# Two encoder layers on one core: the feed-forward input product in Strassen blocks, the output product as a second pass over DRAM

## The chip, the cores and the metric

The kernel runs on one core of one Trainium2 chip. The metric is the device time of one execution in microseconds (us). Engines are TensorE (PE; PEld is its weight load), VectorE (DVE), ScalarE (ACT), GpSimd (POOL) and SyncE (SP, which issues all DMAs of this kernel).

## The reference, cut to what matters

All tensors are float32: 1024 tokens, model width 1024, two layers, feed-forward width 2816.

```python
def conv_ffn(h, w_in, conv_w, conv_b, w_out):          # w_in (1024, 5632), w_out (2816, 1024)
    gu = dwconv_centred(h @ w_in, conv_w, conv_b)      # 3 taps along the tokens, per column, plus bias
    gate, up = split_last(gu, [D_FF, D_FF])
    return (jax.nn.silu(gate) * up) @ w_out
...
    for l in range(DEPTH):
        ...                                            # o: four mixers side by side (attention, scans)
        x = x + rms_norm(o @ w_out[l], post_mix_norm[l])
        h = rms_norm(x, pre_ffn_norm[l])
        x = x + rms_norm(conv_ffn(h, f_w_in[l], f_conv_w[l], f_conv_b[l], f_w_out[l]), post_ffn_norm[l])
```

## The kernel before

One program runs both layers; a layer is the mixers (`mix`), the projection of their output (`out_proj`), and the feed-forward part (`ffn`). Every product of float32 matrices is made of three matmuls on rounded parts: each operand is split into hi (an ACT copy to the fp32r type, L133) and lo (source minus hi, L135, on DVE unless POOL is named), and hi*hi + hi*lo + lo*hi are summed in PSUM. `split` and `splits` do this everywhere, so L133 and L135 are lines of many tiles.

The normalised activations `hn` of a token tile (128 tokens) are transposed on TensorE and split into `hT` (`hT_tile`, L192 to L205): model columns on partitions, tokens along the free axis, in two halves of 512 tokens. Token tiles 0 to 3 are done inside the projection's pipeline; `hn` of tiles 4 to 7 is held and flipped after it (L1463 to L1480).

The feed-forward input product takes the 5632 columns of `w_in` in tiles of 128. For each, `load_T` (L243) loads two raw tiles of 256 KB and splits them, and `gemm_T` (L254) runs 8 row tiles x 3 terms x 2 token halves of matmuls with 512 moving columns into a PSUM tile `pm` of 1024 columns. The first two column tiles of a layer go half by half, so that the first token half is used before the second is there. Column tile f is the gate, 22 + f the matching up tile; `post_gate` and `post_up` run the convolution straight from PSUM (`conv`, L388 to L390: one ACT instruction with tap and bias, two DVE instructions for the neighbours), then tanh on ACT and the gate product (silu as tanh, L320, L321), the product of gate and up (L328), and the split of the result in 256-column parts `gh`, `gl` in SBUF.

The output product is interleaved: after every two pairs, `out_tile` (L348) adds their part of all 8 token tiles, six matmuls of 512 columns for each half of the model width, into two one-bank PSUM tiles, and DVE adds these to the accumulator `acc` (L362). The last group runs through `skew`, a software pipeline, with the layer's tail behind it: `postnorm` (L207), and in the first layer the next layer's `prenorm`, transposes and first column work.

Tiles in SBUF come from pools with tags: `s4` (4 KB per partition, 34 of them), `s2`, `s1`, and `raw` (4 tiles for incoming weights). PSUM has 2 tiles `p2` of two banks, 2 `p1` and 2 `pt` of one bank. A tile waits until one of its tag is free. The instruction order on each engine is set when the program is built, by a planner that takes the instructions in the order in which the code names them as priorities and its own durations; on the chip each engine takes its instructions strictly in that order, and SP its DMA issues too.

```python
class Trunk:
    slots = 34, 12, 24          # s4, s2, s1
...
    def splits(self, *parts, eng=None):
        nc = self.nc
        for hi, lo, src in parts:
            nc.scalar.activation(out=hi, in_=src, func=AF.Copy)
        for hi, lo, src in parts:
            (eng or nc.vector).tensor_tensor(lo, src, hi.bitcast(F32), op=ALU.subtract)
```

## Time and profile before

| | us |
|---|---|
| median of three runs (3164.81 to 3168.3) | 3168.2 |
| the profiled execution, its own time | 3163.46 |
| span of the profiled execution, first to last instruction | 3161.7 |
| TensorE busy in it | 2988.0 |
| mean granted TensorE clock, share of full speed | 0.976 |

The span is read from the trace of the profiled execution. Busy time of an engine is the time in which at least one of its instructions runs; TensorE's matmuls overlap, so the mean duration of one is longer than the distance from one to the next. In the trace, the feed-forward part of layer 1 lies between about 857 and 1600 us, that of layer 2 between about 2420 and the end.

### The profile page before, as it was taken

The numbers are of one execution on the slowest core, as the hardware profiler recorded it, in microseconds if no ns is written. First come the engines' busy times: TensorE is split into PE (matmuls) and PEld (weight loads), VectorE is DVE, ScalarE is ACT, GpSimd is POOL, SyncE is SP. The second block draws the span as 40 slices with busy tenths as digits, with TensorE's granted clock in tenths as the row PEclk, the third lists the DMA queues.
The fourth block names the chain that finished last, engine by engine and source line by source line (L and its number), as shares of the span: only waits on it lengthen the run. The fifth ranks groups of instructions, "written<-read, shape, count | busy, mean of one in ns | idle before, by whom it ended". The sixth has DMA issues, their size and how long they took to land. (4 is left out here: it accounts for less than half of the span.)

```text
span 3161.7 us, 48962 instructions
## 1 busy us (share of the span) xinstructions
PE 2988.0 (95%) x18206; PEld 2493.7 (79%) x18206; DVE 1941.6 (61%) x3654; ACT 1262.7 (40%) x2695; POOL 793.3 (25%) x1257
## 2 busy tenths in 40 slices
PE   6998998999999999999999988999899999999997
PEld 6777776777888888888787777777788888888886
DVE  4556587696545555555565574887955455555556
ACT  3333355785432222222243333577744322222221
POOL 1256667221200000000143675763211000000003
PEclk9999998999999999999999998999999999999999
DMA  4246533233321111111232545232422111111212
GB/s 138 66 144 156 130 88 88 77 102 99 110 66 41 50 59 53 40 41 60 77 126 77 158 131 134 81 92 73 116 94 98 54 57 61 44 40 43 62 36 113
DMA packets 384977, 266.76 MB, mean 84 GB/s; under 512 B 148288, under 2 KB 353636, under 8 KB 384740
## 3 DMA queue, kind: packets, MB, share of 16 engines
q1 hardware_dynamic: 384740, 263.64, 28.7%
q8 instruction: 144, 2.36, 0.3%
q14 instruction: 93, 0.76, 0.1%
HBM read 194.54 MB, written 68.94 MB: 83 GB/s over the span
## 5 line engine op out<-in xcount | busy, mean ns | idle before, releaser
L263 PE MATMUL p<-hT,wh 128*128 128x512 f32 x3456 | 960.1, 392 | 7.8 <-ACT cy L388 2.6
L263 PEld LDWEIGHTS p<-hT,wh 128*128 128x128 f32 x3456 | 649.6, 189 | 145.4 <-ACT cy L388 3.4
L263 PE MATMUL p<-hT,wl 128*128 128x512 f32 x1728 | 553.1, 391 | 0.0
L221 POOL TENSOR_TENSOR acc<-acc,gain 128x768 f32<-128x768 f32 x14 | 28.9, 2064 | 1412.5 <-ACT junk L177 1412.5
L263 PEld LDWEIGHTS p<-hT,wl 128*128 128x128 f32 x1728 | 325.3, 189 | 68.3 <-DVE wl L135 0.9
L388 ACT ACTIVATE cy<-p,cw 128x1024 f32<-128x1024 f32 x88 | 106.0, 1204 | 593.8 <-PE p L263 593.8
L389 DVE SCALAR_TENSOR_TENSOR cy<-p,cw,cy 128x1023 f32<-128x1023 f32 x88 | 112.8, 1282 | 362.3 <-ACT cy L388 362.1
L523 PE MATMUL p<-wn,hT 128*128 128x256 f32 (+1 forms) x1920 | 291.6, 307 | 30.8 <-DVE pb L563 15.5
L523 PEld LDWEIGHTS p<-wn,hT 128*128 128x128 f32 x1920 | 267.5, 199 | 40.9 <-DVE pb L563 17.2
L133 ACT ACTIVATE wh<-raw 128x512 fp32r<-128x512 f32 x216 | 128.0, 624 | 184.1 <-PE p L263 94.6
L135 DVE TENSOR_TENSOR pT<-pt,pT 128x512 fp32r<-128x512 f32 x256 | 173.2, 683 | 39.1 <-ACT pT L133 37.8
L133 ACT ACTIVATE pT<-pt 128x512 fp32r<-128x512 f32 x256 | 150.5, 596 | 96.8 <-PE pt L493 86.8
L493 PE MATMUL pt<-ident,p 128*128 128x128 f32 x1024 | 158.2, 280 | 21.9 <-DVE qh L135 8.2
L362 DVE TENSOR_TENSOR acc<-acc,p 128x512 f32<-128x512 f32 x160 | 109.3, 685 | 93.2 <-PE p L358 93.2
L362 DVE TENSOR_TENSOR acc<-acc,pt 128x512 f32<-128x512 f32 x160 | 109.5, 684 | 90.9 <-PE pt L358 88.9
L1087 DVE TENSOR_REDUCE nm<-p 128x1 f32<-128x1024 f32 x128 | 155.1, 1217 | 13.8 <-PE p L1085 13.2
L1420 PE MATMUL p<-wo,oh 128*128 128x512 f32 x512 | 161.7, 394 | 0.8 <-ACT oh L133 0.8
L493 PEld LDWEIGHTS pt<-ident,p 128*128 128x128 f32 x1024 | 117.4, 142 | 49.0 <-DVE qh L135 11.1
L135 DVE TENSOR_TENSOR wl<-raw,wh 128x512 fp32r<-128x512 f32 x180 | 116.5, 686 | 61.8 <-ACT wh L133 61.6
L1093 ACT ACTIVATE p<-p,nm 128x1024 f32<-128x1024 f32 x128 | 142.3, 1112 | 21.9 <-DVE nm L1087 21.0
L358 PE MATMUL p<-owh,gh 128*128 128x512 f32 x352 | 138.1, 392 | 2.7 <-DVE acc L362 2.7
L358 PE MATMUL pt<-owh,gh 128*128 128x512 f32 x352 | 137.7, 391 | 2.9 <-DVE acc L362 2.8
(317 smaller groups left out, 5624.3 us busy)
## 6 DMA issues: line engine op xcount, KB each, us to landing
raw<-in_f_w_in_dram SPq DMA_DIRECT2D x176, 256.0 KB
raw<-in_f_w_out_dram SPq DMA_DIRECT2D x88, 256.0 KB
raw<-in_w_in_dram SPq DMA_DIRECT2D x72, 256.0 KB
raw<-in_w_out_dram SPq DMA_DIRECT2D x32, 256.0 KB
xr<-x_mid SPq DMA_DIRECT2D x16, 512.0 KB
x_mid<-xr SPq DMA_DIRECT2D x14, 512.0 KB
orow<-o_d SPq DMA_DIRECT2D x48, 128.0 KB
pa<-pa_d SPq DMA_DIRECT2D x32, 176.0 KB
```

Source lines behind the costliest of these rows:

```text
L133: nc.scalar.activation(out=hi, in_=src, func=AF.Copy)
L135: (eng or nc.vector).tensor_tensor(lo, src, hi.bitcast(F32), op=ALU.subtract)
L263: nc.tensor.matmul(pm[:, h * 512:(h + 1) * 512], s[:, k % 4, :], self.h_mov(p, k, h), start=a, stop=b)
L358: nc.tensor.matmul(po, s[i // 2][:, tk], w[:, cs], start=a, stop=b)
L362: nc.vector.tensor_tensor(acc[i][:, cs], acc[i][:, cs], po, op=ALU.add)
L388: nc.scalar.activation(out=y, in_=p, func=AF.Identity, scale=w1, bias=b)
L389: nc.vector.scalar_tensor_tensor(y[:, 1:], p[:, :n - 1], w0, y[:, 1:], op0=ALU.mult, op1=ALU.add)
L493: self.nc.tensor.transpose(pt[:n, t, :], src(4 * c + t), self.ident)
L523: self.nc.tensor.matmul(po, self.h_sta(a, k, i), wt[k][b], start=(k == 0 and a == 0 and b == 0), stop=(k == 7 and a == 1))
L1087: v.reduce_max(nm, s, axis=AX.X, negate=True)
L1093: nc.scalar.activation(out=p, in_=s, func=AF.Exp, bias=nm, accum_out=rs)
L1420: nc.tensor.matmul(y[:, cs], s[k // 2][:, k % 2, :], W[k][w][:, cs], start=(k == 0 and s is oh and w == 0), stop=(k == 7 and s is ol))
```

## The change

The input product is done for a pair (gate tile f, up tile 22 + f) at once, as a product of 2 x 2 blocks: the columns of the pair (gate, up) and the two halves of the 1024 model columns on one side (a11, a12, a21, a22, weight blocks of 512 x 128), the two halves of the model columns and the two token halves on the other (11, 21 for the first token half, 12, 22 for the second). Strassen's scheme in Winograd's form needs 7 block products of 4 x 3 matmuls where 8 were used. Its sums come before and after: the sums of activations (T1 to T4) are made once per layer in `block_tile`, the sums of weight blocks (s1 to s4) for each pair in `pair_pieces` on POOL, and the sums of products partly in PSUM (products added into Q and E) and partly by ACT copies and DVE additions into the SBUF tiles `ug` and `uu`. The convolution then reads these. Each weight piece (hi and lo) is an `s4` tile. Products of a pair and the next are interleaved in the order that `order` writes out; pieces are named up to `piece_ahead` products before their use.

The gated product of each pair goes to a DRAM tile `g_d`. After all 22 pairs, the output product runs as a second pass over blocks of feed-forward tiles, 2, then five times 4: `load_out` loads and splits the weights of the next block, `load_g` reads g back and splits it. The first block uses the small `s1` tiles, with matmuls of 256 columns. The last block is in the pipeline with the layer's tail. There are 38 `s4` tiles in place of 34; a scratch area is set to 1024 bytes.

```diff
@@ -52,7 +52,8 @@
     def t(self, pool, shape, dt, tag, **kw):
         return pool.tile(shape, dt, tag=tag, name=self.nm(tag), **kw)
 
-    slots = 34, 12, 24
+    slots = 38, 12, 24
+    piece_ahead = 3
 
     def setup(self):
         nc = self.nc
@@ -284,15 +285,96 @@
         self.drain(prev)
         yield len(jobs)
 
+    def block_tile(self, i, hn):
+        nc = self.nc
+        v, g = nc.vector, nc.gpsimd
+        half, o = divmod(i, 4)
+        sl = slice(o * 128, (o + 1) * 128)
+
+        def operand():
+            return [[self.s4([128, 2, 512], F32R, "H") for _ in range(2)] for _ in range(2)]
+
+        def put(name, src, eng):
+            hi, lo = self.H[name]
+            self.splits(*((hi[k][:, :, sl], lo[k][:, :, sl], src[:, 2 * k:2 * k + 2, :]) for k in range(2)), eng=eng)
+
+        if i == 0:
+            self.H = {n: operand() for n in ("11", "21")}
+            self.Hraw = [[self.s4([128, 2, 512], nm="Hr") for _ in range(2)] for _ in range(2)]
+        if i == 4:
+            self.H.update({n: operand() for n in ("22", "T1", "T2", "T3", "T4")})
+        pts = []
+        for c in range(2):
+            pt = (self.pt, self.p1)[c * half]([128, 4, 128])
+            for k in range(4):
+                nc.tensor.transpose(pt[:, k, :], hn[:, (4 * c + k) * 128:(4 * c + k + 1) * 128], self.ident)
+            pts.append(pt)
+            if half == 0:
+                put(("11", "21")[c], pt, v)
+                for k in range(2):
+                    nc.scalar.activation(out=self.Hraw[c][k][:, :, sl], in_=pt[:, 2 * k:2 * k + 2, :], func=AF.Copy)
+        if half == 0:
+            return
+        b12, b22 = pts
+        old = lambda c: [r[:, :, sl] for r in self.Hraw[c]]
+        cut = lambda t: [t[:, 2 * k:2 * k + 2, :] for k in range(2)]
+        put("22", b22, v)
+        t1, t2, t3, t4 = (self.s2([128, 4, 128], nm="hc") for _ in range(4))
+        for x, y, z in zip(cut(t1), cut(b12), old(0)):
+            v.tensor_tensor(x, y, z, op=ALU.subtract)
+        v.tensor_tensor(t2, b22, t1, op=ALU.subtract)
+        put("T1", t1, v)
+        put("T2", t2, v)
+        nc.scalar.activation(out=t3, in_=b12, func=AF.Copy)
+        v.tensor_tensor(t3, b22, t3, op=ALU.subtract)
+        put("T3", t3, g)
+        for x, y, z in zip(cut(t4), old(1), cut(t2)):
+            g.tensor_tensor(x, y, z, op=ALU.subtract)
+        put("T4", t4, g)
+
+    def load_pair(self, w, f):
+        raws = []
+        for c0, kh in ((f * 128, 0), (D_FF + f * 128, 0), (D_FF + f * 128, 1), (f * 128, 1)):
+            raw = self.t(self.mem, [128, 4, 128], F32, "raw", bufs=4)
+            self.nc.sync.dma_start(raw, w[kh * 512:(kh + 1) * 512, c0:c0 + 128].rearrange("(k p) c -> p k c", p=128))
+            raws.append(raw)
+        return raws
+
+    def pair_pieces(self, raws):
+        nc = self.nc
+        v, g = nc.vector, nc.gpsimd
+        a11, a21, a22, a12 = raws
+
+        def piece(src, eng):
+            w = self.s4([128, 2, 4, 128], F32R, "wp")
+            self.split(w[:, 0], w[:, 1], src, eng)
+            return w
+
+        def combine(x, y, op):
+            t = self.s2([128, 4, 128], nm="wc")
+            g.tensor_tensor(t, x, y, op=op)
+            return t
+
+        s1 = combine(a21, a22, ALU.add)
+        yield piece(a11, v)
+        yield piece(s1, v)
+        s2 = combine(s1, a11, ALU.subtract)
+        yield piece(a12, v)
+        s4 = combine(a12, s2, ALU.subtract)
+        yield piece(s4, v)
+        s3 = combine(a11, a21, ALU.subtract)
+        yield piece(s2, v)
+        yield piece(s3, g)
+        yield piece(a22, g)
+
     def ffn_first(self, l, P):
-        self.ffn_w = self.load_T(P["f_w_in"][l], 0)
+        self.ffn_w = self.load_pair(P["f_w_in"][l], 0)
 
     def ffn(self, l, P, tail):
         nc = self.nc
+        v = nc.vector
         w_in, w_out = P["f_w_in"][l], P["f_w_out"][l]
-        G = 2
-        NG = NFF // G
-        acc = [None] * NT
+        g_d = self.dr.tile([NFF, 128, L], F32, name=self.nm("g_d"), tag="g_d")
...
+        order = [(0, x) for x in (1, 2, 5, 3, 6)]
+        for f in range(NFF):
+            if f + 1 < NFF:
+                order += [(f + 1, 1), (f, 7), (f + 1, 5), (f, 4), (f + 1, 2), (f + 1, 3), (f + 1, 6)]
+            else:
+                order += [(f, 7), (f, 4)]
+        plan = [(f, x) for f in range(NFF) for x in (1, 5, 2, 3, 6, 7, 4)]
+        made, makers, st = {}, {}, {}
+        raws = {0: self.ffn_w}
+        moving = {1: "11", 5: "T1", 2: "21", 3: "22", 6: "T2", 7: "T3", 4: "T4"}
+
+        def ensure(n):
+            while len(made) < n and plan:
+                f, x = plan.pop(0)
+                if f not in makers:
+                    if f not in raws:
+                        raws[f] = self.load_pair(w_in, f)
+                    makers[f] = self.pair_pieces(raws.pop(f))
+                made[f, x] = next(makers[f])
+
+        def finish(f):
+            ug, uu = st.pop(f)[2:4]
+            y = []
+            for c, u in ((f, ug), (NFF + f, uu)):
+                y.append(self.s4([128, L], nm="cy"))
+                self.conv(y[-1], u, *(cw[:, j, c:c + 1] for j in range(4)))
+                if u is ug:
+                    for h in range(2):
+                        hs = slice(h * 512, (h + 1) * 512)
+                        nc.scalar.activation(out=ug[:, hs], in_=y[0][:, hs], func=AF.Tanh)
+                        v.scalar_tensor_tensor(y[0][:, hs], ug[:, hs], 1.0, y[0][:, hs], op0=ALU.add, op1=ALU.mult)
+            v.tensor_tensor(y[1], y[1], y[0], op=ALU.mult)
+            nc.sync.dma_start(g_d[f], y[1])
+
+        for f, x in order:
+            ensure(self.piece_ahead)
+            w = made.pop((f, x))
+            if x == 1:
+                st[f] = [self.p1([128, 512]), self.p2([128, L]), self.s4([128, L], nm="u"), self.s4([128, L], nm="u"), {}]
+            Q, ER, ug, uu, tmp = st[f]
+            E, R = ER[:, 0:512], ER[:, 512:1024]
+            dst = {5: E, 3: E, 2: R}.get(x, Q)
+            hi, lo = self.H[moving[x]]
+            for k in range(4):
+                for s, (a, m) in enumerate(((0, hi), (0, lo), (1, hi))):
+                    nc.tensor.matmul(dst, w[:, a, k, :], m[k // 2][:, k % 2, :], start=(x in (1, 2, 5) and k == 0 and s == 0),
+                                     stop=(k == 3 and s == 2), skip_group_check=True)
+            if x == 2:
+                tmp["c"] = self.s2([128, 512], nm="p1c")
+                nc.scalar.activation(out=tmp["c"], in_=Q, func=AF.Copy)
+                v.tensor_tensor(ug[:, 0:512], tmp["c"], R, op=ALU.add)
+            if x == 5:
+                tmp["e"] = self.s2([128, 512], nm="ec")
+                nc.scalar.activation(out=tmp["e"], in_=E, func=AF.Copy)
+            if x == 6:
+                tmp["u"] = self.s2([128, 512], nm="uc")
+                nc.scalar.activation(out=tmp["u"], in_=Q, func=AF.Copy)
+                v.tensor_tensor(ug[:, 512:1024], tmp["u"], E, op=ALU.add)
+            if x == 7:
+                v.tensor_tensor(uu[:, 512:1024], tmp["e"], Q, op=ALU.add)
+            if x == 4:
+                nc.scalar.activation(out=uu[:, 0:512], in_=Q, func=AF.Copy)
+                finish(f)
+
+        acc = [None] * NT
+        blocks = [range(0, 2)] + [range(i, i + 4) for i in range(2, NFF, 4)]
+
+        def load_out(f, small):
+            parts = []
             for c in range(2):
-                cs = slice(c * 512, (c + 1) * 512)
                 raw = self.t(self.mem, [128, 512], F32, "raw", bufs=4)
...
+                nc.sync.dma_start(raw, w_out[f * 128:(f + 1) * 128, c * 512:(c + 1) * 512])
+                if small:
+                    for q in range(2):
+                        t = self.s1([128, 256], F32R, "owh"), self.s1([128, 256], F32R, "owl")
+                        self.split(*t, raw[:, q * 256:(q + 1) * 256])
+                        parts.append((c, q * 256, 256, *t))
+                else:
+                    if c == 0:
+                        hl = self.s4([128, DM], F32R, "owh"), self.s4([128, DM], F32R, "owl")
+                    t = [x[:, c * 512:(c + 1) * 512] for x in hl]
+                    self.split(*t, raw)
+                    parts.append((c, 0, 512, *t))
+            return parts
+
+        def load_g(fs, i, small):
+            n, w = len(fs), (128 if small else 256)
+            make = (lambda dt, nm: self.s1([128, 2, 128], dt, nm)) if small else (lambda dt, nm: self.s4([128, 4, 256], dt, nm))
+            raw, hi, lo = make(F32, "gr"), make(F32R, "gh"), make(F32R, "gl")
+            nc.sync.dma_start(raw, g_d[fs[0]:fs[0] + n, :, i * 128:i * 128 + w].rearrange("f p t -> p f t"))
+            self.split(hi, lo, raw)
+            return hi, lo
+
+        def out_tile(bi, i, W, G):
+            fs = blocks[bi]
+            small = len(fs) == 2
+            gh, gl = G[i if small else i // 2]
+            tk = slice(0, 128) if small else slice((i % 2) * 128, (i % 2) * 128 + 128)
+            if bi == 0:
                 acc[i] = self.s4([128, DM], nm="acc")
             for c in range(2):
                 cs = slice(c * 512, (c + 1) * 512)
                 po = (self.p1, self.pt)[c]([128, 512])
...
+                for q in range(2 if small else 1):
+                    for j, f in enumerate(fs):
+                        _, o, n, wh, wl = [x for x in W[f] if x[0] == c][q]
+                        for s, (a, b) in enumerate(((gh, wh), (gh, wl), (gl, wh))):
+                            nc.tensor.matmul(po[:, o:o + n], a[:, j, tk], b, start=(j == 0 and s == 0), stop=(j == len(fs) - 1 and s == 2))
+                if bi == 0:
                     nc.scalar.activation(out=acc[i][:, cs], in_=po, func=AF.Copy)
                 else:
-                    nc.vector.tensor_tensor(acc[i][:, cs], acc[i][:, cs], po, op=ALU.add)
+                    v.tensor_tensor(acc[i][:, cs], acc[i][:, cs], po, op=ALU.add)
             return acc[i]
 
...
+        W = {f: load_out(f, True) for f in blocks[0]}
+        for bi, fs in enumerate(blocks):
+            small = bi == 0
+            step = 1 if small else 2
+            nxt = {}
+            G = {}
+
+            def grab(i):
+                if i < NT and i % step == 0:
+                    G[i // step] = load_g(fs, i, small)
+
+            def tile(i, _=None):
+                if i == 0:
+                    grab(0)
+                grab(i + step)
+                if bi + 1 < len(blocks) and i % 2 == 0:
+                    f = blocks[bi + 1][i // 2]
+                    nxt[f] = load_out(f, False)
+                return out_tile(bi, i, W, G)
+
+            if bi + 1 < len(blocks):
+                for i in range(NT):
+                    tile(i)
+            else:
+                self.drain(self.skew(NT, tile, *tail()))
+            W = nxt
 
     def conv(self, y, p, w0, w1, w2, b=None):
         nc = self.nc
@@ -1462,7 +1611,7 @@
 
         def flip(i, hn):
             if i < 4:
-                self.hT_tile(i, hn)
+                self.block_tile(i, hn)
             else:
                 held.append((i, hn))
 
@@ -1477,7 +1626,7 @@
             if k == self.ffn_at:
                 self.ffn_first(l, P)
         for i, hn in held:
-            self.hT_tile(i, hn, 1)
+            self.block_tile(i, hn)
 
         def end():
             gp = self.bcast_row(P["post_ffn_norm"][l])
@@ -1510,7 +1659,7 @@
     import concourse.bacc as _bacc
     from concourse.bass_utils import run_bass_kernel_spmd as _run
 
-    nc = _bacc.Bacc("TRN2", target_bir_lowering=False, num_devices=1)
+    nc = _bacc.Bacc("TRN2", target_bir_lowering=False, num_devices=1, dynamic_dma_scratch_size=1024)
```

## Rows read from the trace of the kernel before

**Rows 1.** The page, busy time of each engine over the span.

```profile
PE 2988.0 (95%) x18206; PEld 2493.7 (79%) x18206; DVE 1941.6 (61%) x3654; ACT 1262.7 (40%) x2695; POOL 793.3 (25%) x1257
```

**Rows 2.** Stretches of feed-forward layer 1: busy us, (instructions), granted clock, DMA share.

```profile
1000.00:1100.00 100.00, 100.00 (x443) 82.81 (x442) 50.20 (x72) 20.32 (x36) 0.00 (x0) 1.00 0.12 38
...
sum 500.00, PE 500.00 PEld 414.01 DVE 269.33 ACT 121.21 POOL 0.00; mean PE 100.00 PEld 82.80 DVE 53.87 ACT 24.24 POOL 0.00
```

**Rows 3.** Groups by line, TensorE: count, busy us, mean ns, idle before.

```profile
L263 PE MATMUL p<-hT,wh 128*128 128x512 f32 x3456 | 960.1, 392 | 7.8 <-ACT cy L388 2.6 <-ACT wh L133 2.2 <-DVE dy L390 1.7
...
L263 PE MATMUL p<-hT,wl 128*128 128x512 f32 x1728 | 553.1, 391 | 0.0
...
L358 PE MATMUL p<-owh,gh 128*128 128x512 f32 x352 | 138.1, 392 | 2.7 <-DVE acc L362 2.7
```

**Rows 4.** Timeline, attention stage, TensorE: 256-wide products (start, length, count).

```profile
410.06 2.15 PE L1118 MATMUL p<-pT,VA 128*128 128x256 f32 x16
```

**Rows 5.** Groups by line: ACT, DVE and POOL durations of the operations that recur.

```profile
L133 ACT ACTIVATE wh<-raw 128x512 fp32r<-128x512 f32 x216 | 128.0, 624 | 184.1 <-PE p L263 94.6 <-DMA raw<-in_f_w_in_dram 52.7 <-issue 17.0
...
L135 DVE TENSOR_TENSOR wl<-raw,wh 128x512 fp32r<-128x512 f32 x180 | 116.5, 686 | 61.8 <-ACT wh L133 61.6
...
L389 DVE SCALAR_TENSOR_TENSOR cy<-p,cw,cy 128x1023 f32<-128x1023 f32 x88 | 112.8, 1282 | 362.3 <-ACT cy L388 362.1
...
L362 DVE TENSOR_TENSOR acc<-acc,p 128x512 f32<-128x512 f32 x160 | 109.3, 685 | 93.2 <-PE p L358 93.2
L388 ACT ACTIVATE cy<-p,cw 128x1024 f32<-128x1024 f32 x88 | 106.0, 1204 | 593.8 <-PE p L263 593.8
...
L321 DVE SCALAR_TENSOR_TENSOR cy<-th,cy 128x512 f32<-128x512 f32 x88 | 56.9, 688 | 31.8 <-ACT th L320 31.8
...
L328 DVE TENSOR_TENSOR cy<-cy,cy 128x1024 f32<-128x1024 f32 x44 | 53.6, 1219 | 0.1
...
L135 POOL TENSOR_TENSOR wl<-raw,wh 128x512 fp32r<-128x512 f32 x36 | 47.7, 1328 | 78.1 <-ACT wh L133 75.0 <-DMA pa_d<-pa 3.0
...
L741 POOL TENSOR_TENSOR X<-xs,dt 128x256 f32<-128x256 f32 x60 | 39.7, 671 | 41.6 <-PE p L767 40.8 <-DVE X L764 0.9
```

**Rows 6.** Timeline, end of layer 1: DVE, POOL and a TensorE wait.

```profile
1570.44 1.85 POOL L221 TENSOR_TENSOR acc<-acc,gain 128x768 f32<-128x768 f32 x1 [706.26 <-ACT junk L177]
...
1570.81 0.69 DVE L362 TENSOR_TENSOR acc<-acc,pt 128x512 f32<-128x512 f32 x1 [1.70 <-PE pt L358]
...
1574.49 2.07 POOL L221 TENSOR_TENSOR acc<-acc,gain 128x768 f32<-128x768 f32 x1 [1.24 <-ACT junk L177]
...
1574.79 2.86 DVE L226 SCALAR_TENSOR_TENSOR xr<-acc,rs,xr 128x1024 f32<-128x1024 f32 x1
...
1577.57 1.27 DVE L362 TENSOR_TENSOR acc<-acc,p 128x512 f32<-128x512 f32 x2
...
1578.30 0.50 PE L358 MATMUL p<-owh,gh 128*128 128x512 f32 x1 [2.04 <-DVE acc L362]
...
1578.76 1.27 DVE L226 SCALAR_TENSOR_TENSOR xr<-acc,rs,xr 128x1024 f32<-128x1024 f32 x1
```

**Rows 7.** Timeline, start of feed-forward layer 1.

```profile
855.71 0.39 PE L1420 MATMUL p<-wo,ol 128*128 128x512 f32 x1
...
857.17 0.70 PE L263 MATMUL p<-hT,wh 128*128 128x512 f32 x2
...
871.14 1.41 DVE L135 TENSOR_TENSOR hT<-p,hT 128x256 fp32r<-128x256 f32 x4
```

**Rows 8.** Stretches at the start and the end of feed-forward layer 1.

```profile
860.00:880.00 20.00, 19.59 (x95) 15.90 (x93) 12.71 (x27) 9.30 (x25) 2.52 (x3) 1.00 0.44 132
...
1570.00:1580.00 10.00, 7.96 (x34) 6.22 (x33) 8.59 (x9) 3.71 (x8) 7.43 (x7) 0.98 0.43 123
1580.00:1590.00 10.00, 7.67 (x33) 6.29 (x32) 9.29 (x10) 4.66 (x10) 8.85 (x12) 0.83 0.54 195
```

**Rows 9.** Timeline, the program's last TensorE instruction.

```profile
3147.69 0.63 PE L358 MATMUL pt<-owh,gl 128*128 128x512 f32 x1
```

More of the change, by code (lines that the diff above doesn't have):

```diff
@@ L324, in post_up @@
-        def post_up(f, pm):
-            y = side(pm, NFF + f)
-            yield
-            g = gate.pop(f)
-            nc.vector.tensor_tensor(y, y, g, op=ALU.mult)
-            gh, gl = [], []
-            for c in range(4):
-                a, b = self.s1([128, 256], F32R, "gh"), self.s1([128, 256], F32R, "gl")
-                self.split(a, b, y[:, c * 256:(c + 1) * 256])
-                gh.append(a)
-                gl.append(b)
-            gT[f] = gh, gl
-        def load_out(f):
-            wh = self.s4([128, DM], F32R, "owh")
-            wl = self.s4([128, DM], F32R, "owl")
+        order = [(0, x) for x in (1, 2, 5, 3, 6)]
@@ L369, in ffn @@
-        per = 2 * G
-        for i in self.run_T(jobs, self.ffn_w):
-            gi, r = divmod(i, per)
-            if r == 0 and gi < NG:
-                for j in range(G):
-                    load_out(gi * G + j)
-            if r == 1 and 0 < gi < NG:
-                for tk in range(NT // 2 if gi == NG - 1 else NT):
-                    out_tile(gi - 1, tk)
-        for tk in range(NT // 2, NT):
-            out_tile(NG - 2, tk)
-        self.drain(self.skew(NT, lambda i, _: out_tile(NG - 1, i), *tail()))
+        W = {f: load_out(f, True) for f in blocks[0]}
```

30 lines of the change are left out of this document (removed).

## The prediction

> **What bounds the kernel now.** I read the page first: TensorE is busy 95% of the span, VectorE (DVE) 61%, ScalarE (ACT) 40%, GpSimd (POOL) 25% [rows 1]. Shares over a span hide stages, so I then took the middle of one feed-forward layer in stretches of 100 us. There TensorE is busy for 500.00 of 500 us at full clock, while DVE has half of its time free, ACT three quarters, and POOL does nothing; the DMA engines are busy 12 to 20% [rows 2]. The reader is to see two things. Only fewer or shorter matmuls can shorten this stage; and the stage has much idle time on the other engines, so work may be added there as long as it does not become the longer queue. The groups by line give the matmul groups concerned, their idle time before is 8 us out of some 1,500 [rows 3]. The pitch follows from the count: 443 matmuls of 512 columns in 100 us, 0.226 us each [rows 2].
>
> **The change on TensorE.** The input product of a layer has 44 column tiles x 8 row tiles x 3 (hi and lo terms) x 2 token halves = 2112 matmuls of 512 columns, the output product 22 x 8 x 2 x 3 = 1056. After the change the input product has 22 pairs x 7 products x 4 x 3 = 1848. The output product keeps its work, but the first block of two tiles runs in 256-column halves: 192 such matmuls in place of 96. So 264 + 96 = 360 matmuls x 0.226 = 81.4 us go. The 256-column ones take (2.15 - 0.28)/15 = 0.125 us each where sixteen of them run in a row [rows 4] (0.28, the length of one, stands at the end of the run); 192 x 0.125 = 24.0 come. Net -57.4 per layer, **-115 us** for both. Nothing hides this: it is the bound itself.
>
> **The change on the other engines, first pass.** TensorE needs 84 x 0.226 = 18.98 us for a pair of tiles f. In that time, by busy time over count [rows 5]:
>
> - ACT: seven hi copies of 0.62 (weight pieces), four PSUM copies priced alike, two biased copies of 1.20, two tanh priced like the copies of 512: 10.5 us. Hidden.
> - DVE: five lo subtractions 5 x 0.647 = 3.24, four convolution steps 4 x 1.28 = 5.13, two gate products 1.29, one product 1.22: 10.9 us with both tensors in SBUF. Three sums with one tensor in PSUM at L362's 0.68: 2.05. Together 12.9 us.
> - POOL: four sums of weight blocks and two lo subtractions, 512 wide. By L135 1.33 each; by the 768-wide L221, 1.85 [rows 6], two thirds of it, 1.23. So 7.4 to 8.0 us.
>
> Each fits below 18.98 by itself. But the timeline at the end of the layer shows that DVE and POOL do not run side by side [rows 6]. A DVE L226, both tensors in SBUF, starts at 1574.79 while POOL's L221 runs from 1574.49 to 1576.56, and takes 2.86 us; alone, at 1578.76, it takes 1.27. DVE's L362, which reads a PSUM tile, takes its ordinary 0.69 at 1570.81 although POOL runs until 1572.29. So a DVE instruction with two SBUF tensors waits for the POOL instruction to end, and one with a PSUM tensor does not. What is behind it waits as well: the L362 pair of 1577.57 is late, and TensorE sits idle 2.04 us for it at 1578.30. Before, the feed-forward stage had no POOL work, and its convolution read PSUM; after, the convolution reads the sums u in SBUF, and POOL has six instructions per pair. This is where the change can lose what it wins.
>
> The time of a pair by these rows: below, if DVE's PSUM sums always fall under a POOL instruction, 10.9 + 7.4 = 18.3, which TensorE's 18.98 covers; above, if POOL never overlaps with DVE, 12.9 + 7.4 = 20.3 (20.9 with the dear POOL price). Only 2.05 of 12.9 us of DVE's work may overlap, and DVE takes its instructions in order, so I take 20.3: 1.32 us per pair over TensorE's pace, x 44 pairs = **+58 us**. TensorE feels it in two places: a weight piece whose lo part is late, and product 4 of a pair, which overwrites Q only after DVE has read Q for uu, with one product (12 x 0.226 = 2.7 us) of cover.
>
> [...]
>
> **Start of the layer.** Before, 48 matmuls on the first token half (10.9 us) cover the second half's transposes and splits: the last matmul of the projection starts at 855.71, the feed-forward one at 857.17, the last split of the second half ends at 872.55 [rows 7], and TensorE loses 0.4 us there [rows 8]. After, only products 1 and 2 need the first half alone: 24 matmuls, 5.4 us of cover, 5.4 less. Each of the four late token tiles costs DVE six splits and two subtractions of 256 and two subtractions of 512 (priced by columns from L135, 0.33 and 0.65): 3.9 us, where it were four splits, 1.3; 10.4 us more for four tiles. They cannot be spread over the projection: of 38 big slots, its weights hold 16, H11, H21 and Hraw 12, two gains 2, and the 20 new slots come free only as its last matmuls run. DVE has 7 us free in that stretch [rows 8]. So 5.4 + 10.4 = 15.8 at most and, with part of the free time used, I take 13 per layer, **+26** (bounds 10 and 36, the upper with 2 us of halved clock per layer after the gap: rows 8 show 0.83 in such a stretch).
>
> **Second pass.** Blocks of four tiles have 192 matmuls, 43.4 us. DVE has 8 x 0.65 (weights) + 4 x 1.22 (g) + 16 x 0.68 = 21 us, ACT 10, POOL nothing: hidden. Writing and rereading g adds 23 MB per layer, some 35 GB/s over 660 us, beside 195 GB/s that a stretch of before moved [rows 8]; hidden, and priced at nothing while g is written a block ahead. The first block is the exception: 24 us, 16 accumulator copies and ten weight and g copies on ACT (some 20 us), small slots for two g tiles ahead. I take 3 us per layer, **+6** (bounds 0 and 20).
>
> **End of the layer.** The last group now gives 24 matmuls, 5.4 us, to each token tile in place of 12; the post-norm chain, which made TensorE idle 2.0 of 10 and 2.3 of 10 us [rows 8], then has more cover, and the drain after the last matmul (3147.7 to the span's end at 3161.7 [rows 9]) holds fewer tiles. I take **-9** for both layers (bounds 0 and -16).
>
> **Sum.** The profiled execution took 3163.46 us. 3163.5 - 115 + 26 + 58 + 6 - 9 = 3129.5. The three runs shown have a median of 3168.2, 4.7 above; I forecast **3134 us**.
>
> **Rivals.**
>
> 1. TensorE stays the bound in the first pass, since the sums fall under POOL and slack in the slots smooths the rest (18.3 of 18.98 us). For it: DVE can run three instructions of a pair beside POOL. Against: 96% use without queueing. It takes the 58 away: 3076. Chance 0.21.
> 2. It ends slower. Same place, one step more: each of the four combined pieces goes POOL, ACT, DVE, and if DVE stands idle for the ACT copy (0.62), a pair takes up to 20.3 + 2.5 = 22.8 us, +110: 3244; with two of four exposed 3189. The gain is used up at 18.98 + (115 - 26 - 6 + 9)/44 = 21.07 us per pair. For it: DVE and ACT take their queues in order, and DVE's idle time in today's kernel is nearly all a wait for ACT (L389 and L135) [rows 5]. Against: pieces are made up to three products ahead. Chance 0.19.
> 3. Loads come late. The write of g waits for the last product of a pair's tail on the one DMA-issuing queue, and the raw tiles of the next pair stand behind it, with four buffers only. From product 4 the tail takes 0.6 + 1.2 + 2.6 + 1.2 = 5.6 us unhindered, and the next pair's first product comes 3 products, 8.1 us, later; if the loads land 2.5 us too late each time, that is 44 x 2.5 = 110 without the 58: 3186. Chance 0.07.
>
> **How the numbers follow.** The forecast case, 20.3 us per pair or near it (3095 to 3160), has 0.45; the case that the gain is just used up, within 0.2% (6 us, about what a measurement of this kernel can tell), 0.08. Faster: 0.45 + 0.21 = 0.66; same 0.08; slower 0.19 + 0.07 = 0.26. The range goes from the first rival with a better end, 3070, to 21.9 us per pair, 3205, rounded to 3210; what lies outside is some 0.05 below and 0.12 above.
>
> **What would show it.** TensorE's counts: 1848 products, 960 of 512 and 192 of 256 columns per layer. In the first pass TensorE under full busy time (some 94%), its idle time ended by DVE's piece or sum, and DVE instructions of 1.28 us alone that take up to 2.5 beside POOL. In the second pass 500 of 500 as before. A gap of some 10 us at each layer's start. If TensorE is full in the first pass, rival 1 holds; if its waits end in ACT copies or loads, 2 or 3. Wrong altogether would be a start or a first block that costs more than 50 us, or a halved clock through the first pass.

## The result, and the profile after

The changed kernel takes 3240.34 us (median of 4 runs), the kernel before 3167.32 us: ratio 1.0237, 95% interval [1.0207, 1.0266]. It is slower by 73 us, where 3134 us were forecast. The profiled execution took 3251.27 us, 87.8 more than that of before. It is the longest of the four (3235.84 to 3251.27) and 10.9 us over their median, that of before 3.9 under its own: so 15 of the 87.8 us are scatter between executions.

The page after, engines' busy time (beside [rows 1]) and four of its groups:

```profile
PE 2947.6 (91%) x17870; PEld 2427.9 (75%) x17870; DVE 2216.8 (68%) x3606; ACT 1450.4 (45%) x2979; POOL 1298.1 (40%) x1569
...
L435 PE MATMUL p<-H,wp 128*128 128x512 f32 x3696 | 878.9, 396 | 90.8 <-DVE wp L136 48.3
...
L539 DVE SCALAR_TENSOR_TENSOR cy<-u,cw,cy 128x1023 f32<-128x1023 f32 x88 | 153.9, 1749 | 1.5
...
L420 DVE SCALAR_TENSOR_TENSOR cy<-u,cy 128x512 f32<-128x512 f32 x88 | 144.4, 1680 | 3.6 <-ACT u L419 3.6
```

TensorE has 336 instructions less and 40 us less busy time, but the first pass (L435) stands still for 90.8 us, 48.3 of them for a weight piece's lo part; the input product of before stood 7.8 us [rows 3]. The second convolution step L539 takes 1.75 us for the 1.28 of [rows 5], and the gate product L420 takes 1.68 for the 0.69 of L321 [rows 5].

The middle of the first pass of layer 1 in the changed kernel, as a window to set beside [rows 2]:

```profile
1100.00:1300.00 200.00, 181.10 (x772) 141.78 (x771) 167.51 (x141) 85.59 (x136) 99.31 (x55) 1.00 0.23 74
```

TensorE's two waits in this stretch, and the longest of DVE, POOL and ACT (us in total, times, longest):

```profile
PE p L435 <- DVE wp L136: 11.5, 10, 1.2
PE p L435 <- ACT wp L134: 7.4, 9, 0.8
...
DVE wp L136 <- ACT wp L134: 27.9, 9, 3.1
POOL wp L136 <- ACT wp L134: 95.9, 9, 10.7
ACT ec L443 <- PE p L435: 48.9, 9, 5.5
```

No engine is full, and the clock is 1.00. Ten waits in 200 us means one of each kind per pair: a ring of dependences, not an engine, sets the pace. TensorE waits for the parts of a piece, DVE and POOL wait for ACT's hi copy of it, and ACT waits for TensorE: its copies of E (L443) and of Q (L446, another 43.4 us in 9 waits) stand in its queue until their product is done, with hi copies behind them. No wait of any engine in this stretch ends in a load. The product of gate and up (L421) starts every 21.7 us, pair after pair. The timeline of one such pair, POOL first (start, length, count, idle before):

```profile
1112.05 2.00 POOL L136 TENSOR_TENSOR wp<-wc,wp 128x512 fp32r<-128x512 f32 x1 [10.68 <-ACT wp L134]
1114.01 1.73 POOL L136 TENSOR_TENSOR wp<-raw,wp 128x512 fp32r<-128x512 f32 x1
1115.70 1.74 POOL L355 TENSOR_TENSOR wc<-raw,raw 128x512 f32<-128x512 f32 x1
1117.52 2.16 POOL L355 TENSOR_TENSOR wc<-wc,raw 128x512 f32<-128x512 f32 x1
1119.76 1.63 POOL L355 TENSOR_TENSOR wc<-raw,wc 128x512 f32<-128x512 f32 x1
1121.35 1.74 POOL L355 TENSOR_TENSOR wc<-raw,raw 128x512 f32<-128x512 f32 x1
```

The same stretch of the timeline on DVE, and where TensorE goes on:

```profile
1107.97 0.69 DVE L136 TENSOR_TENSOR wp<-wc,wp 128x512 fp32r<-128x512 f32 x1 [3.11 <-ACT wp L134]
...
1110.42 1.28 DVE L539 SCALAR_TENSOR_TENSOR cy<-u,cw,cy 128x1023 f32<-128x1023 f32 x1
...
1116.22 2.31 DVE L539 SCALAR_TENSOR_TENSOR cy<-u,cw,cy 128x1023 f32<-128x1023 f32 x1
1118.45 3.49 DVE L420 SCALAR_TENSOR_TENSOR cy<-u,cy 128x512 f32<-128x512 f32 x2
1121.97 2.20 DVE L421 TENSOR_TENSOR cy<-cy,cy 128x1024 f32<-128x1024 f32 x1
1124.10 0.67 DVE L447 TENSOR_TENSOR u<-uc,p 128x512 f32<-128x512 f32 x1
1124.69 0.68 DVE L136 TENSOR_TENSOR wp<-wc,wp 128x512 fp32r<-128x512 f32 x1
...
1125.43 8.50 PE L435 MATMUL p<-H,wp 128*128 128x512 f32 x36 [1.18 <-DVE wp L136]
```

POOL idles 10.68 us, then does its six instructions in one burst of 11 us. DVE works undisturbed (1.28) until the burst, and inside it the instructions with two SBUF tensors are stretched: 2.31 us for the L539 at 1116.22, 3.49 for two of L420, 2.20 for L421. The sum L440, which reads PSUM, keeps its 0.68 in the burst (at 1112.82). The piece's lo part at 1124.69 stands behind L421, and TensorE waits 1.18 us for it (it goes on at 1125.43).

The start of layer 1 (windows as in [rows 8]); the last projection matmul starts at 876.53, the first product at 899.84:

```profile
880.00:900.00 20.00, 5.04 (x19) 3.52 (x19) 19.39 (x37) 14.34 (x42) 13.96 (x19) 0.51 0.07 27
900.00:920.00 20.00, 16.18 (x41) 11.71 (x42) 11.29 (x14) 7.52 (x16) 18.57 (x17) 0.63 0.18 53
```

DVE is full for the 20 us in which TensorE does almost nothing; after that gap the granted clock is 0.63 (0.50 from 900 to 904 and from 908 to 916), and 41 matmuls take 16.18 us of busy time, 0.39 each for the 0.226 of [rows 2]. DVE's splits of T1 and T2, which have both inputs in SBUF, are stretched here too, since POOL works on T3 and T4 at the same time:

```profile
888.34 0.74 DVE L136 TENSOR_TENSOR H<-hc,H 128x256 fp32r<-128x256 f32 x2
...
892.25 4.53 POOL L136 TENSOR_TENSOR H<-hc,H 128x256 fp32r<-128x256 f32 x5
...
895.26 1.80 DVE L136 TENSOR_TENSOR H<-hc,H 128x256 fp32r<-128x256 f32 x2
```

At 888.34 POOL stands idle; the seven other such rows of the four held tiles take 1.28 to 1.83 us, 5.0 us more in all than at 0.74.

All stages, in us of the profiled executions, cut at the starts of TensorE's last projection matmul and last output matmul of each layer in the timelines. In brackets stand the gap ahead of the first product and the pass from its first to its last product; labels are those of the experiments:

| | mixers 1 | ffn 1 (gap + first pass) | mixers 2 | ffn 2 with drain (gap + first pass) |
|---|---|---|---|---|
| before | 855.7 | 755.9 | 808.6 | 741.5 |
| after | 876.5 | 791.6 (23.3 + 493.3) | 812.3 | 769.1 (23.3 + 490.6) |
| e2_before_slots | 865.8 | 754.1 | 815.4 | 741.5 |
| e3_second_pass | 866.1 | 758.5 (1.5 + 482.8) | 812.7 | 737.9 (1.5 + 482.8) |
| e1_pool_to_dve | 867.2 | 757.5 (23.3 + 457.9) | 816.3 | 737.5 (23.3 + 457.7) |
| e12_after_ahead4 | 867.9 | 730.3 (23.3 + 432.2) | 809.6 | 716.6 (23.3 + 437.6) |
| e14_ahead4_timed | 868.3 | 724.8 (23.3 + 430.7) | 809.6 | 709.7 (23.3 + 431.6) |

### The profile page after: what moved, and what is told of

It is laid out like the page before. It is cut to its first block, busy times and chain, and to the rows that moved or that the text cites. A ratio compares the mean times of both kernels' runs of the same rounds, so it can differ in the third digit from the quotient of the medians.

```text
span 3249.5 us, 49308 instructions
## 1 busy us (share of the span) xinstructions
PE 2947.6 (91%) x17870; PEld 2427.9 (75%) x17870; DVE 2216.8 (68%) x3606; ACT 1450.4 (45%) x2979; POOL 1298.1 (40%) x1569
## 5 line engine op out<-in xcount | busy, mean ns | idle before, releaser
L435 PE MATMUL p<-H,wp 128*128 128x512 f32 x3696 | 878.9, 396 | 90.8 <-DVE wp L136 48.3
L435 PEld LDWEIGHTS p<-H,wp 128*128 128x128 f32 x3696 | 687.1, 190 | 280.8 <-DVE wp L136 66.1
L136 POOL TENSOR_TENSOR wp<-wc,wp 128x512 fp32r<-128x512 f32 x44 | 86.1, 1957 | 455.9 <-ACT wp L134 455.9
L136 DVE TENSOR_TENSOR wp<-wc,wp 128x512 fp32r<-128x512 f32 x132 | 115.9, 880 | 142.0 <-ACT wp L134 142.0
L136 DVE TENSOR_TENSOR pT<-pt,pT 128x512 fp32r<-128x512 f32 x256 | 173.5, 683 | 40.4 <-ACT pT L134 38.7
L264 PE MATMUL p<-hT,wh 128*128 128x512 f32 x640 | 190.8, 410 | 5.7 <-ACT wh L134 2.2
L497 PE MATMUL p<-owh,gh 128*128 128x512 f32 (+1 forms) x384 | 145.8, 380 | 17.2 <-ACT gh L134 11.9
L539 DVE SCALAR_TENSOR_TENSOR cy<-u,cw,cy 128x1023 f32<-128x1023 f32 x88 | 153.9, 1749 | 1.5
L355 POOL TENSOR_TENSOR wc<-raw,raw 128x512 f32<-128x512 f32 x88 | 150.3, 1708 | 2.2 <-DMA raw<-in_f_w_in_dram 2.2
L264 PEld LDWEIGHTS p<-hT,wh 128*128 128x128 f32 x640 | 124.2, 197 | 33.6 <-ACT wh L134 2.8
L420 DVE SCALAR_TENSOR_TENSOR cy<-u,cy 128x512 f32<-128x512 f32 x88 | 144.4, 1680 | 3.6 <-ACT u L419 3.6
L497 PE MATMUL pt<-owh,gh 128*128 128x512 f32 (+1 forms) x384 | 145.2, 378 | 0.0
```

What stands on the lines that cost most here:

```text
L264: nc.tensor.matmul(pm[:, h * 512:(h + 1) * 512], s[:, k % 4, :], self.h_mov(p, k, h), start=a, stop=b)
L355: g.tensor_tensor(t, x, y, op=op)
L420: v.scalar_tensor_tensor(y[0][:, hs], ug[:, hs], 1.0, y[0][:, hs], op0=ALU.add, op1=ALU.mult)
L435: nc.tensor.matmul(dst, w[:, a, k, :], m[k // 2][:, k % 2, :], start=(x in (1, 2, 5) and k == 0 and s == 0), stop=(k == 3 and s == 2), ski ...
L497: nc.tensor.matmul(po[:, o:o + n], a[:, j, tk], b, start=(j == 0 and s == 0), stop=(j == len(fs) - 1 and s == 2))
L539: nc.vector.scalar_tensor_tensor(y[:, :n - 1], p[:, 1:], w2, y[:, :n - 1], op0=ALU.mult, op1=ALU.add)
```

## The experiments

The first theory was the prediction's mechanism: DVE and POOL exclude each other, read from [rows 6] (2.86 us for 1.27), and so a pair costs 21.7 us. The rival: the pieces come too late for another reason (their order, ACT's copies, the start).

**1. POOL's six instructions of a pair put on DVE.**

```diff
-            g.tensor_tensor(t, x, y, op=op)
+            v.tensor_tensor(t, x, y, op=op)
...
-        yield piece(s3, g)
-        yield piece(a22, g)
+        yield piece(s3, v)
+        yield piece(a22, v)
```

> The six POOL instructions of a pair (four sums of weight blocks, two lo subtractions) are moved to DVE; POOL has nothing to do in the first pass. Theory A, DVE and POOL exclude each other and the burst of six POOL instructions stretches DVE's: DVE then has 12.9 + 6 x 0.65 = 16.8 us per pair, under TensorE's 18.98, a pair takes 19.0 to 19.6 us instead of 21.7, and the time falls by 90 to 115 us, to about 3135. Theory B, the order of ACT's queue (hi copies of pieces stand behind a copy that waits for TensorE) sets the 21.7: a pair takes 21.5 or more, since DVE has more work behind the same chain, and the time is 3235 to 3290.

3172.46 us, 68 less than the change and between the two theories. The pair takes 20.2 us. The same window of e1:

```profile
1100.00:1300.00 200.00, 191.72 (x831) 153.31 (x830) 155.62 (x207) 94.39 (x150) 0.00 (x0) 1.00 0.24 77
```

TensorE's only wait in it:

```profile
PE p L435 <- ACT wp L134: 8.3, 10, 0.8
```

DVE is busy for less time although it does more. POOL's part costs something, then, by the exclusion or by POOL's longer instructions (1.33 us for DVE's 0.69 at L135, the means of one in [rows 5]); but TensorE still lacks 8 us in 200, with DVE 44 us idle.

**2. POOL's instructions as memsets.** Each of the six is two memsets (0.53 us each, same tiles and queue). The weight sums and the lo parts of two pieces are left out.

> Each of the six POOL instructions of a pair is replaced by two POOL memsets of the same tile, which write but read nothing: the sums of weight blocks and two lo parts are left out, the output is not the reference's, the number of waits on POOL is kept. Theory A in its narrow form (only a POOL instruction that reads SBUF keeps out DVE's two-tensor instructions): DVE's instructions keep their lengths alone, a pair takes 19.0 to 19.8 us, the time is about 3140. If a POOL instruction of any kind keeps DVE out, or if the order of the queues is the cause (theory B), a pair takes 21 us or more and the time is 3210 or more.

3177.27 us (one run), pair 20.2 us, again between the two times expected. A group of the stretch from 1100 to 1300, then the second convolution step, which is L545 in this kernel, as a group and in the timeline beside the memsets:

```profile
L361 POOL MEMSET wc<- 128x512 f32 x80 | 38.1, 530 | 0.0
...
L545 DVE SCALAR_TENSOR_TENSOR cy<-u,cw,cy 128x1023 f32<-128x1023 f32 x20 | 25.6, 1282 | 0.4
...
1106.29 1.28 DVE L545 SCALAR_TENSOR_TENSOR cy<-u,cw,cy 128x1023 f32<-128x1023 f32 x1
...
1106.36 3.81 POOL L361 MEMSET wc<- 128x512 f32 x8
```

POOL is busy, with instructions that write SBUF but read none of it, and the convolution step keeps its 1.28 even in the midst of them. So POOL's writing alone does not stretch DVE here; beside POOL's sums and subtractions, which read SBUF too, the same step took 1.80 in this stretch of the changed kernel. The pair is as long as in e1, and TensorE's only wait is the same 8.3 us for ACT. POOL works for 57 us of the 200 here, for 99 in the changed kernel, so the run does not part what the stretch costs from what POOL's own longer work costs.

**3. Sizes alone, and the second pass alone.** The first is the kernel before with `slots = 38, 12, 24` and the DMA scratch of after; the second adds to it g through DRAM and the second pass, with the input product of before.

> The kernel before with only the sizes of after: 38 big slots in place of 34 and the scratch area of 1024 bytes. In the trace of after, the first layer's projection starts 20.7 us later than before, and the second layer's mixers take 11 us less, though their code is the same. If the sizes change the planned order of the mixers, this kernel is 5 to 25 us slower than before (3172 to 3192) and shows the same later start; if the difference is one of the executions, it stays within 0.2% of 3167.

> The second pass alone: the input product as before (8 products, convolution from PSUM), the gated product to DRAM, the output product in blocks of 2, 4, 4, 4, 4, 4, with the sizes of after. TensorE's work changes by 192 x 0.125 - 96 x 0.226 = +2.3 us per layer. If the second pass is hidden as predicted (+3 per first block, -4.5 per tail), the time is that of the kernel with the new sizes alone within 10 us. If it loses what the trace of after suggests (the stretches of its first 40 us show 8 us without TensorE and a clock of 0.9), the time is 20 to 50 us above it.

3179.64 us, ratio 1.0044 [1.0027, 1.0060], and 3182.94 us, ratio 1.0052 [1.0035, 1.0069]. The sizes move next to nothing in the feed-forward stages (1.8 us less in layer 1); they lengthen the mixers, whose code is the same: 865.8 + 815.4 for 855.7 + 808.6 in the table. Each engine's order is planned when the program is built, and with other sizes the plan comes out different: in the traces of before and e2 DVE's first 224 instructions come in the same order, and then the orders part. Which of the two sizes does it was not tried. My expectation read 11 us less for the second layer's mixers in the changed kernel; by the table they take 3.7 us more. The second pass is hidden.

**4. The order of ACT's copies, the start, the gate.** Three edits on top of e1: the copy of product 1 is named right behind it; the four held token tiles are named behind the first two products; and (on top of the first of these) the gate's convolution is named after product 6.

```diff
-            if x == 2:
+            if x == 1:
                 tmp["c"] = self.s2([128, 512], nm="p1c")
                 nc.scalar.activation(out=tmp["c"], in_=Q, func=AF.Copy)
+            if x == 2:
```

> POOL's six instructions on DVE as in the first experiment, and the ACT copy of Q (p1c) is named right after product 1 of a pair instead of after product 2. With POOL empty a pair takes 20.23 us, and TensorE waits 0.8 us per pair for a hi copy of ACT. Theory A2, ACT takes its queue in order and the hi copies stand in a burst behind the copy of E, for which ACT waits 6.4 us: the burst of 6.1 us after product 5 has 5.4 us of cover; without p1c (0.59) it is 5.5, a pair takes 19.5 to 19.8 us, the time falls by 20 to 30 us against the first experiment (3172). Theory B2, the hi copies wait for a big slot: a pair stays at 20.2 us, the time within 6 us of 3172.

```diff
+            if (f, x) == (0, 5):
+                for i, hn in self.held:
+                    self.block_tile(i, hn)
```

> POOL's six instructions on DVE, and the held token tiles are named after products 1 and 2 of the first pair instead of before them. Today 23.3 us pass between the last matmul of the projection and the first product of a layer. Theory A3, the first products stand behind the held tiles for their PSUM tile and in the order of DVE and ACT, not for data: the first product starts 10 to 20 us earlier, the 24 products (5.4 us, at the halved clock 10) fall into the gap, and each layer wins 5 to 12 us, 10 to 25 in all against 3172. Rival, DVE is full from the first held tile on and the pieces of the first products push its work back by as much: the win is under 5 us.

> As the experiment with the early copy of Q, and the gate's convolution, tanh and product are named after product 6 of a pair, not after product 4. Theory A2: one of the two biased copies of 1.24 us leaves ACT's burst too, TensorE's waits go, a pair takes 18.98 to 19.3 us, the time falls by 40 to 55 us against 3172. Theory B2: the gate tile takes a big slot earlier, pieces come later, a pair takes 20.2 us or more.

3176.16, 3180.43 and 3210.18 us: none helps. The first moves the 0.8 us wait from ACT's piece to DVE's, the pair stays at 20.2 us. The second closes the gap from 23.3 to 6.7 us and pays it back in the pass (457.9 to 471.7): the start is bound by DVE's work on the token tiles, wherever the products stand. The third makes the pair 21.1 us.

**5. A lead of four pieces.** `ensure(self.piece_ahead)` names weight pieces until three are made and unused.

```diff
-    piece_ahead = 3
+    piece_ahead = 4
```

On e1, in two runs:

> POOL's six instructions on DVE, pieces named 4 products ahead instead of 3. Theory B2 (big slots are given in the order of the code, and pieces come after the pair's sums): pieces get their slots earlier, a pair takes 19.6 us or less, the time is 3145 or less. Theory A2: the hi copies keep their place behind the copy of E, a pair stays at 20.0 to 20.3, the time within 10 us of 3172.

> Sums on DVE and a lead of four once more, for an interval. If the lead is what sets the pair, 3105 to 3115 us and a ratio of 0.981 to 0.984 against the kernel before; if the single time of the first look was a lucky one, 3125 us or more.

3109.96 us, then 3113.65 us: ratio 0.9834 [0.9818, 0.9850] against the kernel before, the best of all. On the changed kernel itself, POOL's work where it was:

> The changed kernel with POOL's work where it was, and only the lead of the weight pieces raised from three to four. Exclusion theory: POOL's burst and DVE's work go one after the other, whatever the lead. A pair then wants DVE's own 12.5 us (124 of 200 us busy at 20.2 us a pair, in the run whose POOL work was memsets) and POOL's 7.4 to 8 us unhindered, together 20 to 20.5 us; so the pair stays at 20 to 21.7 us, the first pass at 455 to 493 us a layer, and the time at 3170 to 3240 us. Rival, that the short lead alone made the loss and the exclusion is covered once pieces are early: pair 18.98 us as with the work on DVE and a lead of four, first pass 431 us, time 3110 to 3125 us.

3126.38 us, ratio 0.9877 [0.9853, 0.9900]: the first theory falls. POOL's six instructions stay, and one number takes 114 us away. The same window of e12:

```profile
1100.00:1300.00 200.00, 200.00 (x884) 165.67 (x884) 171.72 (x157) 97.09 (x153) 120.53 (x65) 1.00 0.26 83
```

Two of its groups by line in that stretch (the convolution step, and POOL's sums of two raw tiles):

```profile
L539 DVE SCALAR_TENSOR_TENSOR cy<-u,cw,cy 128x1023 f32<-128x1023 f32 x21 | 39.3, 1871 | 0.4
L355 POOL TENSOR_TENSOR wc<-raw,raw 128x512 f32<-128x512 f32 x21 | 32.6, 1554 | 45.8 <-DMA raw<-in_f_w_in_dram 27.6 <-PE p L435 9.7 <-DVE cy L539 8.6
```

L539 is stretched more than in the changed kernel (1.87 us for 1.80 in this stretch, 1.28 in e1), and TensorE is full, 19.0 us a pair. The gate product is hardly stretched any more:

```profile
L420 DVE SCALAR_TENSOR_TENSOR cy<-u,cy 128x512 f32<-128x512 f32 x20 | 13.5, 718 | 15.3 <-ACT u L419 15.3
```

It took 1.78 us in the same stretch of the changed kernel. In all, DVE is busy for 16.3 us of a pair here, 18.2 in the changed kernel and some 12.5 beside the memsets of e7; so some two thirds of the stretch are left, and they cost nothing in this stretch, because no product waits for them. The waits that closed the ring are nearly gone: ACT waits 6.3 us for product 5 (L443) and 5.3 for product 6 (L446), where it waited 48.9 and 43.4, and DVE waits for no hi copy. My expectation had added all of DVE's 12.5 us to POOL's 7.4 to 8; the sums that read PSUM need no turn: L440, L447 and L449 take 0.67 to 0.69 in this stretch, as L362 takes 0.69 beside POOL in [rows 6].

| us, median (pair) | lead 3 | lead 4 |
|---|---|---|
| six instructions on POOL | 3240.34 (21.7) | 3126.38 (19.0) |
| the same on DVE | 3172.46 (20.2) | 3113.65 (19.0) |

Two variants of the lead of four with DVE: a lead of five, and the start of e9.

> Sums on DVE and a lead of five. If a lead of four already hides all of DVE's and ACT's work, nothing changes: pair 18.98 us, 3105 to 3115 us. Rival, that the fifth piece takes a big slot which the accumulators' copies or the convolution's results need: pair over 19.5 us, 3125 us or more.

> Lead of four, sums on DVE, and the four held token tiles put behind the first two products. If the start is bound by DVE's work (as with a lead of three, where the gap fell by 16.6 us and the rest of the pass grew by 13.8 us): some 3 us a layer, 3100 to 3107 us. Rival, that with a longer lead DVE's work in the first pairs is off the path and the gap is won: 16.6 us a layer, 3077 us. The order could also cost the lead in the first pairs: 3110 us or more.

3118.83 and 3119.11 us; neither gains. In the second the gap is 7.3 us and the pass 446.6, together 453.9 for the 454.0 of e14: all that the gap gives is paid back.

**6. Which pieces are late.** Counted in products of the code's order, with a lead of three the piece of product 1 is named 0 products ahead, that of 5 one, of 2, 3 and 6 two, of 7 three, of 4 four: the plan goes pair by pair, and names 7 and 4 ahead of the next pair's 1. First, naming in the products' order (`plan = list(order)`), two ahead for all. In the first pair the pieces of products 2 and 5 change places by it, so these three kernels compute something else there; the pairs behind it are as they should be.

> The changed kernel, lead of three and GpSimd's work kept; alone the order in which the pieces are named is now that of the products. In the changed kernel products 1 and 5 of the next pair get their pieces named with no lead, since those of products 7 and 4 stand ahead of them in the plan. Theory that this order made the loss: the pair falls from 21.7 us to under 19.5 us, the first pass to 432 to 445 us a layer, the time to 3120 to 3150 us. Rival, that three pieces in flight are too few in any order beside GpSimd's burst: pair over 20.5 us, time 3190 us or more.

> The same order of naming, lead of three, with GpSimd's six instructions of a pair on VectorE. Order theory: from 20.23 us a pair to 18.98 to 19.3 us, first pass 431 to 438 us, time 3110 to 3130 us. Rival, too few in flight: it stays at 20 us or more, 3165 us or more.

> Both: pieces named in the products' order and a lead of four, GpSimd's work on VectorE. If TensorE already bounds the pair with a lead of four, order adds nothing: pair 18.98 us, 3105 to 3120 us. Rival, that the other order makes a new wait (the piece of product 4 later than before): 3125 us or more.

3225.29, 3217.28 and 3162.51 us: against the same kernels with the old plan 15 less, 45 more and 49 more. It is no cure. Then the one product of lead split between the pieces:

```diff
-            ensure(self.piece_ahead)
+            ensure(4 if x in (6, 1) else 3)
```

names 1 and 5 one product earlier; `3 if x in (6, 1) else 4` is the complement, and the last run is the first edit on e1.

> The changed kernel, with a lead of four only while products 6 and 1 are named, so that the pieces of products 1 and 5 of the next pair come one product earlier and all others as before. Theory that these two are the late ones: pair under 19.5 us, first pass 432 to 445 us, time 3125 to 3155 us, most of what a lead of four gave. Rival, that the other pieces (those of 2, 3 and 6 above all, named behind the last product's convolution) are the late ones: pair over 20.8 us, time 3200 us or more.

> The complement: one product more of lead for products 7, 4, 2, 3 and 6, none for 1 and 5. Theory that 1 and 5 are the late ones: the pair stays near 21.7 us, time 3210 to 3240 us. Rival, that the others are: pair under 19.5 us, time 3125 to 3155 us. Between them, if each of the pieces adds its share.

> A lead of four for products 1 and 5 alone, with GpSimd's work on VectorE. Theory that these two are late: pair 18.98 to 19.3 us instead of 20.23 us, time 3110 to 3125 us. Rival: 20 us a pair as before, 3165 us or more.

3287.88, 3127.26 and 3209.63 us. The pieces of 7, 4, 2, 3 and 6 are the late ones: their one product gives all that the lead of four gave (3126.38). Those of 1 and 5 do harm when they come earlier, 48 us with POOL and 37 without. POOL's longest wait in e19 (1100 to 1300):

```profile
POOL wc L355 <- DMA raw<-in_f_w_in_dram: 92.0, 17, 12.1
```

POOL's only wait in e20, same stretch:

```profile
POOL wp L136 <- ACT wp L134: 80.0, 11, 7.3
```

In e19 a weight sum stands at the head of POOL's queue and waits up to 12.1 us for its load, with whatever is queued behind it; in e20 no sum waits for a load there. The loads stand on SP behind the write of g (L422). SP's wait for that write's data in the changed kernel:

```profile
SPq L422 <- DVE cy L421: 80.4, 10, 8.0
```

and in e20:

```profile
SPq L422 <- DVE cy L421: 32.2, 11, 2.9
```

For e19 this fits a second ring: a late product makes g late, g holds the loads, the loads hold the pieces. It is not the ring of the changed kernel, where no sum waits for a load in this stretch; there it runs through ACT, as shown with the result. Nor is a wait for loads harmful by itself, or g the only thing that holds them: in e12 POOL's sums wait up to 5.4 us for loads with TensorE full, and in the changed kernel SP stands as long for a raw tile to come free behind POOL's L136:

```profile
POOL wc L355 <- DMA raw<-in_f_w_in_dram: 36.9, 17, 5.4
...
SPq L339 <- POOL wp L136: 82.5, 9, 9.3
```

A longer lead names a piece earlier in the engines' queues and also earlier in the order in which the big slots are given out. No run parts these two, none cuts one of the rings alone, and which of the five pieces counts was not tried.

## Why the prediction was wrong, by its own steps

Against the profiled execution of before the sum was 34 us less; it came out 87.8 more (73 by the medians). By the table of stages, with e14 as the kernel whose pairs run at TensorE's pace:

| term | forecast | measured | from |
|---|---|---|---|
| input product, 528 matmuls x 0.226 | -119.3 | -119.3 | taken: the count and pitch of e12's stretch |
| second pass (256-wide included) and end | +1.6 (4.6 + 6 - 9) | -1.0 | ffn, e3 less before |
| start of both layers | +26 | +57.4 | ffn, e14 less e3 (-61.9), + 119.3 |
| pairs over TensorE's pace | +58 | +126.2 | ffn, after less e14 |
| mixers | 0 | +24.5 | after less before |
| sum | -33.7 | +87.8 | |

- **TensorE.** Right. With early pieces 884 matmuls run in 200 us, the pitch of [rows 2].
- **The pair.** This step failed. It priced a pair as a sum of busy times, 20.3 us, as if DVE and POOL took turns without loss. Their turns were seen rightly: in e12, beside POOL's six instructions, the convolution step L539 takes 1.87 us for 1.28. But with the lead of four the six instructions on POOL, turns included, cost only about 13 us (3126.38 against 3113.65). What set 21.7 us was the lead, in the argument that I used against rival 2: "pieces are made up to three products ahead". Counted in the code, five of the seven come two products ahead or less; one product more for those of 7, 4, 2, 3 and 6 brings the pair to TensorE's pace (e20). Of the 126.2 us, the 21 intervals a layer from one L421 to the next make 112 (904.3 in the changed kernel, 792.3 in e14); the rest lies at the ends of the pass and behind it. Rival 2, chance 0.19, had the place and the range (3189 to 3244): DVE stands idle for ACT's hi copies, 27.9 us in the stretch or 3.1 a pair, where it priced up to 2.5. It took this for the fixed length of a chain; with the lead of four the wait is gone. With the lead of three, POOL's place and lateness add to each other: on POOL the six instructions cost 68 us, with four 13.
- **The start.** The place was right, the term less than half of what it came to: +57.4 for +26, both layers together (the row is a remainder: it holds all that e14 loses outside its pairs). The upper bound, 36 for both, did not hold, and 57.4 is past the 50 us that the prediction itself named as wrong altogether. Shown instead: a gap of 23.3 us per layer for 1.5, with DVE full in it, and slow matmuls behind it (0.39 us for 0.226; the bound had 2 us per layer for these, 41 of them alone lose 6.9). DVE's work there was priced by columns alone; the exclusion that the prediction saw for the pairs it left out here, where the T1 and T2 splits beside POOL's work take 5.0 us a layer more than at 0.74 each. Whether the gap shrinks by that much without POOL's part was not tried.
- **The mixers.** Put at nothing without a reason: slot counts were priced only where their tiles are used. In the profiles it is +24.5. With the sizes alone they lengthen by 16.9, and in the other kernels of the table with 38 slots by 13.2 to 19.2. What the changed kernel has beyond that is its profiled execution: up to 840 us DVE, ACT and TensorE take the same instructions in the same order as in e1, and still layer 1's mixers take 876.5 us for 867.2.
- **Second pass, end, loads.** Right: hidden in e3. Rival 3 (loads behind the write of g) was not the cause in the changed kernel, where no engine waits for a load in the stretch, although SP stands 8 us a pair for L421 there; in e19 POOL waits for loads.

That e12 lands near the forecast (3126.38 for 3134) does not save it: it gets there with pairs at TensorE's pace, a start twice as dear and longer mixers.

## What to carry to other kernels

When an edit puts a chain of small preparations (sum, hi copy, lo part) in front of each matmul group, count from the code how many groups ahead each one is named and what long work stands between, before adding up busy times; in the changed kernel a ring of waits set the pace (21.7 us a pair) while no engine was full (TensorE 181.1 us of 200). Test the lead first: it is one number, and here it was worth more than moving the work to another engine (114 us against 68). Run the old kernel with the new buffer counts too, since a plan made at build time moves stages that the edit does not touch.

## What the runs showed of the hardware that I had not expected

POOL instructions that only write SBUF did not stretch DVE: 120 memsets in 200 us left the second convolution step at 1.282 us (e7), where POOL's two-tensor sums made it 1.80 in the changed kernel and 1.87 in e12. And the stretch cost nothing where it was covered: in e12 DVE and POOL show 171.7 and 120.5 us busy in 200 us, the stretch included, and TensorE stands for none of it.
